# Where weight parts, x and the inner activations start within an SBUF partition: other pads in a split-fp32 transformer kernel

## The chip, the cores and the metric

The kernel runs on one core of one Trainium2 chip, in one launch. The metric is the device time of that launch in microseconds (us).

## What is computed

Two blocks follow each other on 256 tokens of width 1024. The first has two layers of feed-forward, mixer, feed-forward; the second has a two-directional recurrent mixer and a layer of retrieved experts. Cut to what matters:

```
x = x + 0.5 * swiglu(rmsnorm(x, g1), w_gate, w_up, w_down)      # D_FF = 2816, twice a layer, 2 layers
x = x + concat(attn_a, attn_b, attn_c)(rmsnorm(x, g) @ w_in) @ w_out
x = x + 0.5 * swiglu(rmsnorm(x, g2), ...)
...
x = x + g1 * token_mixer(norm(x), norm(ctx))                    # second block, one layer
x = x + g2 * peer_ffn(norm(x))     # 8 heads choose 16 of 128 x 128 experts each:
                                   # sum of g * gelu(u_tab[idx] . x) * v_tab[idx]
return rms_norm(x, norm_f_g)
```

The result is compared in fp32, and the kernel computes the experts densely: all 16,384 rows of `u_tab` and `v_tab` are multiplied, and a matrix of gates picks what counts.

## The kernel before

**One product, three matmuls.** fp32 weights come from DRAM in pieces of 128 x 1024 (`raw`, five buffers, class `W`). ScalarE rounds a piece to fp32r (`wH`, line 218), VectorE takes the rest (`wL`, line 219), three buffers each. Activations are split likewise, into `xH` and `xL` (`split_scaled`), `hH` and `hL` (`ffn`), `cH` and `cL` (the context) or the two halves of `hl` (experts). `mm3` then issues three matmuls for each product: line 256 moves the high activations against `wH`, line 257 the low ones against `wH`, line 258 the high ones against `wL`. A matmul has a weight tile of 128 x 128 as its stationary operand and moves 256 columns, the tokens. `mm3t` (lines 265 to 267) has the roles the other way round: x is stationary, and 320 to 512 columns of weights move.

**Stages.** `run` goes through feed-forward `ffn1` and mixer of layer 0, `ffn2` of layer 0, `ffn1` and mixer of layer 1, `ffn2` of layer 1 (with the context's side work between), the second block's mixer (`latents`), and `peer`. A feed-forward first makes 22 pairs of gate and up columns (moving x; 22 x 48 matmuls), which leave `hH[:, j]` and `hL[:, j]`, then 8 output tiles over 22 inner tiles (moving h; 528 matmuls). `peer` makes queries and chooses experts while 64 `u_chunk`s of 48 matmuls move x, and ends with 64 `v_chunk`s of 48 matmuls that move `hl`.

**Order.** The code order is the order on each engine; loads go out on SP's queue, whose order is that of the code too. The side work of a feed-forward (the modulation's products) is a generator that is advanced after inner tile j > 2 and after output tiles; `hold` puts a one-element POOL copy ahead of its loads, so that they start no earlier than a given tile.

**Where a tile starts.** Tiles come from stacked pools, each pool a range of bytes in every partition, and every tile starts at a multiple of 32 bytes. `pad` takes some bytes at the start of a pool, so that what follows moves up: 96 in `s` (small things; `xH` and `xL` in the pool `b` behind it move with it), 32 in `w` (weight parts; all pools behind it move too) and 32 in `po2` (the experts' `hl` and one-hot tiles). The built program has these starts:

| tile | before, modulo 128 | before, modulo 256 | after, modulo 128 | after, modulo 256 |
|---|---|---|---|---|
| `wH`, `wL`, `raw` | 96 | 224 | 0 | 0 |
| `xH`, `xL` | 32 | 160 | 0 | 128 |
| `hH`, `hL` in order of the four calls | 32, 32, 32, 32 | 32, 32, 32, 32 | 64, 96, 0, 64 | 64, 96, 128, 64 |
| `hl` | 32 | 32 | 64 | 64 |
| `oH`, `oL` (mixers' output) | 32 | 32 | 64 | 64 |
| `cH`, `cL` | 96 | 96 | 0 | 128 |

All slices of one tile that a matmul reads start a multiple of 512 bytes apart, so the table holds for every matmul of a tile.

Of the kernel before, what the change touches and what calls it, by code (L numbers as in the profile page):

```python
# [241 lines left out]
class K:  # L242
# [142 lines left out]
        self.consts.append((self.segs[i], t))  # L385


    def ffn(self, name, l, side=iter(()), every=1, down=1):

        nc, x = self.nc, self.x  # L390
        xs = self.split_scaled(x, self.c("g_" + name, KT * l, KT * l + KT), KT)
        rb, _ = self.stats(x, KT, D)
        with self.tc.tile_pool(name="ffn", bufs=1) as fp:
            self.fp = fp
            hH = fp.tile([128, FT, T], F32R, name="hH")
            hL = fp.tile([128, FT, T], F32R, name="hL")
            for j in range(FT):
                w, self.ahead = self.ahead or W(self, self.ap[name + "_gu"][l, j], 2048, 1024), None
                w.load()
                p = self.bank().rearrange("p (a t) -> p a t", a=2)  # L400
                for a in range(2):
                    for k in range(KT):
                        self.mm3(p[:, a], w, (a * KT + k) * 128, xs, k, k == 0, k == KT - 1)
                gu = fp.tile([128, 2, T], F32, name="gu", bufs=2)
                nc.vector.tensor_tensor(gu, p, rb[:, None, :].to_broadcast([128, 2, T]), op=OP.mult)
                nc.scalar.activation(gu[:, 0], gu[:, 0], AF.Silu)
                h = gu[:, 0]
                nc.vector.tensor_tensor(h, h, gu[:, 1], op=OP.mult)
                nc.scalar.activation(hH[:, j], h, AF.Copy)
                nc.vector.tensor_tensor(hL[:, j], h, hH[:, j].bitcast(F32), op=OP.subtract)  # L410
                self.mark = h
                if j % every == 0 and j > 2:
                    self.used_late()
                    next(side, None)
                self.mark = None
            for m in range(KT):
                p = self.bank()[:, :T]
                for half in range(2):
                    w = self.wchunk(self.ap[name + "_d"][l, 2 * m + half], 1408, 768)
                    for k in range(11):  # L420
                        self.mm3(p, w, k * 128, (hH, hL), 11 * half + k, half + k == 0, half * 11 + k == FT - 1)
                nc.vector.scalar_tensor_tensor(x[:, m], p, 0.5, x[:, m], op0=OP.mult, op1=OP.add)
                self.mark = x[:, m]
                self.used_late()
                if down:
                    next(side, None)
                self.mark = None
            self.used_late()
# [1082 lines left out]
    def run(self):  # L1511
        tc, nc = self.tc, self.nc
        with ExitStack() as es:
            self.sp = es.enter_context(tc.tile_pool(name="s", bufs=1))
            self.bp = es.enter_context(tc.tile_pool(name="b", bufs=1))
            self.wp = es.enter_context(tc.tile_pool(name="w", bufs=1))
            dp = es.enter_context(tc.tile_pool(name="d", bufs=1, space=bass.MemoryType.DRAM))
            self.xd = dp.tile([128, KT, T], F32, name="xd")
            self.pad(self.sp, 96)
            self.pad(self.wp, 32)  # L1520
            self.ones = self.sp.tile([128, 128], F32, name="ones")
            nc.vector.memset(self.ones, 1.0)
            with tc.tile_pool(name="x", bufs=1) as xp, tc.tile_pool(name="q", bufs=1) as self.qp:
                self.x = xp.tile([128, KT, T], F32, name="x")
                self.load_consts(self.sp, 0)
                self.ahead = W(self, self.ap["ffn1_gu"][0, 0], 2048, 512)
                for k in range(0, KT, 2):
                    if k % 4 == 0:
                        self.ahead.load(1)
                    nc.sync.dma_start(self.x[:, k:k + 2], self.ap["xT"][:, T * k:T * k + 2 * T])  # L1530
                self.ident = self.c("ident")
                self.mod = self.sp.tile([128, 48, 2], F32, name="mod")
                self.banks = {"mm": 2, "at": 2, "s": 2, "pt": 1, "o": 1}
                with tc.tile_pool(name="g", bufs=1) as gp, \
                        tc.tile_pool(name="ps", bufs=1, space=bass.MemoryType.PSUM) as self.ps:
                    steps = self.modulation(gp)
                    side = chain(islice(steps, 6), self.later(lambda: self.load_consts(gp, 1)), steps)
                    for l in range(2):
                        if l:
                            self.ffn("ffn2", 0, side, 2, 1)  # L1540
                        self.ffn("ffn1", l, side, 2 - l, l)
                        with tc.tile_pool(name="mix", bufs=1) as self.kp:
                            self.mixer(l)
                    for _ in side:
                        pass
                with tc.tile_pool(name="g2", bufs=1) as self.g2:
                    self.banks = {"mm": 3, "at": 3, "c": 2}
                    with tc.tile_pool(name="ps1", bufs=1, space=bass.MemoryType.PSUM) as self.ps:
                        self.pb = "c"
                        with tc.tile_pool(name="ctx", bufs=1) as self.kp:  # L1550
                            side = self.context()
                            self.ffn("ffn2", 1, islice(side, STEPS))
                            xs = self.first_norm()
                            for _ in side:
                                pass
                        self.pb = "mm"
                        self.latents(xs)
                self.banks = {"mm": 4, "at": 4}
            with tc.tile_pool(name="ps2", bufs=1, space=bass.MemoryType.PSUM) as self.ps:
                self.peer()  # L1560
# [33 lines left out]
```

## Time and profile before

| | us |
|---|---|
| three runs | 2116.16, 2124.03, 2128.60 |
| median | 2124.03 |
| the profiled execution | 2126.69 |
| its span, first to last instruction | 2124.8 |

The profile gives busy times by engine, groups of equal instructions, waits, and the instructions in order of time. PE is the matmuls, PEld the weight loads that run beside them. Matmuls are pipelined: one is recorded for some 280 ns while the next starts some 115 ns later, so what counts for the time is the distance from start to start, which the timeline shows directly, or a dense stretch's length divided by the matmuls in it. A window's count includes matmuls that began before it and reach into it.

### The profile page before, as it was taken

How to read it: one execution, taken by the hardware profiler on the slowest of the kernel's cores; microseconds unless marked ns; L12 is line 12 of the kernel's file. 1: busy time of each engine (PE TensorE's matmuls, PEld its weight loads, DVE VectorE, ACT ScalarE, POOL GpSimd, SP SyncE). 2: the span in 40 equal slices, each digit the busy share in tenths (PEclk: the TensorE clock that was granted, in tenths of full speed). 3: DMA queues.
4: the chain of work that ended last, by engine and by line, in shares of the span. 5: the costliest groups of instructions: out<-in, count | busy, mean ns of one | idle time of the engine just before them, and what ended most of it. 6: DMA issues, size and time to landing. Idle time of an engine off the chain costs nothing. (4 is left out here: it accounts for less than half of the span.)

```text
span 2124.8 us, 43280 instructions
## 1 busy us (share of the span) xinstructions
PE 2069.4 (97%) x17204; PEld 2011.8 (95%) x17204; DVE 1590.4 (75%) x3211; ACT 1161.3 (55%) x2011; POOL 38.9 (2%) x148
## 2 busy tenths in 40 slices
PE   8999999999999999999999998999999999999997
PEld 8999989999999998998997898999999999999997
DVE  7776977888787797777758868888888885555555
ACT  5544465444444445557446645545588874444444
POOL 0001000001000100000000000000000000000000
PEclk9999999999999999999999999999999999999998
DMA  7666535768777753555463434555545455555553
GB/s 233 224 211 189 155 101 165 227 215 256 237 261 252 246 161 95 162 182 168 154 194 119 146 113 154 187 193 181 171 160 166 163 170 188 189 186 185 186 188 120
DMA packets 115115, 385.38 MB, mean 181 GB/s; under 512 B 12768, under 2 KB 13920, under 8 KB 114784
## 3 DMA queue, kind: packets, MB, share of 16 engines
q1 hardware_dynamic: 114912, 382.61, 56.0%
q8 instruction: 135, 2.21, 0.4%
q14 instruction: 68, 0.56, 0.1%
HBM read 380.46 MB, written 2.10 MB: 180 GB/s over the span
## 5 line engine op out<-in xcount | busy, mean ns | idle before, releaser
L219 DVE TENSOR_TENSOR wL<-raw,wH 128x1024 fp32r<-128x1024 f32 (+3 forms) x716 | 812.5, 1138 | 368.5 <-ACT wH L218 366.7
L218 ACT ACTIVATE wH<-raw 128x1024 fp32r<-128x1024 f32 (+3 forms) x716 | 707.2, 990 | 679.4 <-PE mm L257 464.2
L256 PE MATMUL mm<-xH,wH 128*128 128x256 f32 x2952 | 833.3, 283 | 10.1 <-ACT xH L360 6.2
L258 PE MATMUL mm<-xH,wL 128*128 128x256 f32 x2952 | 828.7, 281 | 7.4 <-DVE wL L219 7.2
L257 PE MATMUL mm<-xL,wH 128*128 128x256 f32 x2952 | 828.3, 281 | 1.1 <-DVE xL L361 0.5
L256 PEld LDWEIGHTS mm<-xH,wH 128*128 128x128 f32 x2952 | 558.8, 189 | 13.4 <-ACT xH L360 6.7
L258 PEld LDWEIGHTS mm<-xH,wL 128*128 128x128 f32 x2952 | 561.3, 190 | 10.2 <-DVE wL L219 9.1
L257 PEld LDWEIGHTS mm<-xL,wH 128*128 128x128 f32 x2952 | 560.3, 190 | 4.2 <-DVE xL L361 1.8
L257 PE MATMUL mm<-hl,wH 128*128 128x256 f32 x1024 | 286.7, 280 | 0.0
L256 PE MATMUL mm<-hl,wH 128*128 128x256 f32 x1024 | 285.7, 279 | 0.0
L258 PE MATMUL mm<-hl,wL 128*128 128x256 f32 x1024 | 285.7, 279 | 0.0
L258 PE MATMUL mm<-hH,wL 128*128 128x256 f32 x704 | 196.8, 280 | 1.2 <-DVE wL L219 1.2
L257 PE MATMUL mm<-hL,wH 128*128 128x256 f32 x704 | 196.8, 280 | 0.0
L256 PE MATMUL mm<-hH,wH 128*128 128x256 f32 x704 | 196.6, 279 | 0.0
L256 PEld LDWEIGHTS mm<-hl,wH 128*128 128x128 f32 x1024 | 192.5, 188 | 0.0
L257 PEld LDWEIGHTS mm<-hl,wH 128*128 128x128 f32 x1024 | 192.2, 188 | 0.0
L258 PEld LDWEIGHTS mm<-hl,wL 128*128 128x128 f32 x1024 | 191.5, 187 | 0.0
L258 PEld LDWEIGHTS mm<-hH,wL 128*128 128x128 f32 x704 | 131.9, 187 | 1.6 <-DVE wL L219 1.6
L256 PEld LDWEIGHTS mm<-hH,wH 128*128 128x128 f32 x704 | 132.1, 188 | 0.0
L257 PEld LDWEIGHTS mm<-hL,wH 128*128 128x128 f32 x704 | 132.1, 188 | 0.0
L740 DVE SCALAR_TENSOR_TENSOR prod<-wm,cv 128x1024 f32<-128x1024 f32 x64 | 78.4, 1226 | 31.6 <-DMA wm<-wmod 17.4
L1339 ACT ACTIVATE o<-o,gL 128x128 f16<-128x128 f16 x256 | 85.7, 434 | 11.3 <-DVE o L1333 8.0
(466 smaller groups left out, 2507.6 us busy)
## 6 DMA issues: line engine op xcount, KB each, us to landing
raw<-ffn_gu SPq DMA_DIRECT2D x174, 512.0 KB, 4.7
raw<-ut SPq DMA_DIRECT2D x128, 512.0 KB, 4.1
raw<-vt SPq DMA_DIRECT2D x128, 512.0 KB, 4.0
raw<-win SPq DMA_DIRECT2D x58, 512.0 KB, 4.6
wm<-wmod SPq DMA_DIRECT2D x48, 512.0 KB, 5.3
raw<-ffn_d SPq DMA_DIRECT2D x64, 384.0 KB, 3.5
raw<-ffn_d SPq DMA_DIRECT2D x64, 320.0 KB, 3.3
raw<-wout SPq DMA_DIRECT2D x24, 512.0 KB, 3.7
```

The costliest lines, as they stand in the source:

```text
L218: k.nc.scalar.activation(H[:, :n], raw[:, :n], AF.Copy)
L219: k.nc.vector.tensor_tensor(L[:, :n], raw[:, :n], H[:, :n].bitcast(F32), op=OP.subtract)
L256: mm(out, H, xH[:, k], start=first, stop=False, skip_group_check=skip)
L257: mm(out, H, xL[:, k], start=False, stop=False, skip_group_check=skip)
L258: mm(out, L, xH[:, k], start=False, stop=last, skip_group_check=skip)
L740: nc.vector.scalar_tensor_tensor(out, raw, 1.0, cv[:, D * i:D * i + D], op0=OP.mult, op1=OP.mult, accum_out=self.mod[:, j, i:i + 1])
L1339: nc.scalar.activation(o[:, 3, i // 2, :, i % 2], o[:, 1, i // 2, :, i % 2], AF.Copy, scale=wL[:, 4 * u + i:4 * u + i + 1])
```

## The change

`ffn` gets an argument `pad`, and takes that many bytes at the start of its pool: none in the first and the last call, 32 in `ffn2` of layer 0, 64 in `ffn1` of layer 1. The pad of `s` goes from 96 to 64 bytes, that of `w` from 32 to 96. The table above has what that makes of the starts. Nothing else is changed; the memset that fills a pad is the only instruction that is added, two of them.

```diff
-    def ffn(self, name, l, side=iter(()), every=1, down=1):
+    def ffn(self, name, l, side=iter(()), every=1, down=1, pad=0):
...
         with self.tc.tile_pool(name="ffn", bufs=1) as fp:
             self.fp = fp
+            if pad:
+                self.pad(fp, pad)
             hH = fp.tile([128, FT, T], F32R, name="hH")
             hL = fp.tile([128, FT, T], F32R, name="hL")
...
-            self.pad(self.sp, 96)
-            self.pad(self.wp, 32)
+            self.pad(self.sp, 64)
+            self.pad(self.wp, 96)
...
                     for l in range(2):
                         if l:
-                            self.ffn("ffn2", 0, side, 2, 1)
-                        self.ffn("ffn1", l, side, 2 - l, l)
+                            self.ffn("ffn2", 0, side, 2, 1, 32)
+                        self.ffn("ffn1", l, side, 2 - l, l, 64 * l)
```

POOL's instructions where `ffn2` of layer 0 ends and `ffn1` of layer 1 begins (`wm` and `prod` are the modulation's tiles that `hold` marks, `x` and `gu` what they are held for), the program after against the one before:

```order
 L378 COPY prod<-x 128x1
 L378 COPY wm<-x 128x1
+L373 MEMSET pad_6777 128x16
 L378 COPY wm<-gu 128x1
 L378 COPY prod<-gu 128x1
```

The line with + is the pad of `ffn1` of layer 1; `ffn2` of layer 0 has its own further up in the same way, between `kc<-kr` and `wm<-gu`. On PE, VectorE, ScalarE and SP the order of instructions is the same as before.

## Rows read from the trace of the kernel before

**Rows 1.** The page: busy time of each engine; TensorE's granted clock by slice.

```profile
PE 2069.4 (97%) x17204; PEld 2011.8 (95%) x17204; DVE 1590.4 (75%) x3211; ACT 1161.3 (55%) x2011; POOL 38.9 (2%) x148
PEclk9999999999999999999999999999999999999998
```

**Rows 2.** Groups kept apart by form: count, busy us and mean ns, idle before.

```profile
L256 PE MATMUL mm<-xH,wH 128*128 128x256 f32 x2952 | 833.3, 283 | 10.1 <-ACT xH L360 6.2 <-DVE x L709 1.3 <-ACT wH L218 0.8
L256 PE MATMUL at<-xH,wH 128*128 128x256 f32 x128 | 35.8, 285 | 1.7 <-ACT xH L792 1.7
L219 DVE TENSOR_TENSOR wL<-raw,wH 128x1024 fp32r<-128x1024 f32 x546 | 665.7, 1222 | 298.6 <-ACT wH L218 297.9
L256 PE MATMUL mm<-hl,wH 128*128 128x256 f32 x1024 | 285.7, 279 | 0.0
L256 PE MATMUL mm<-hH,wH 128*128 128x256 f32 x704 | 196.6, 279 | 0.0
```

**Rows 3.** Dense stretches of x, PE alone: us, busy (matmuls), clock, DMA share, GB/s.

```profile
24.00:132.00 108.00, 108.00 (x956) 1.00 0.68 222
355.00:471.00 116.00, 116.00 (x987) 1.00 0.68 219
548.00:607.00 59.00, 59.00 (x503) 1.00 0.72 242
888.00:924.00 36.00, 36.00 (x309) 1.00 0.65 224
1344.00:1364.00 20.00, 20.00 (x179) 1.00 0.53 175
1431.00:1457.00 26.00, 26.00 (x223) 1.00 0.56 184
...
1557.00:1743.00 186.00, 128.04 (x463) 1.00 0.50 165
```

**Rows 4.** Groups in 1344 to 1364 us, then in 548 to 607 us.

```profile
L257 PE MATMUL mm<-xL,wH 128*128 128x256 f32 x59 | 16.3, 276 | 0.0
...
L257 PE MATMUL mm<-xL,wH 128*128 128x256 f32 x168 | 47.2, 281 | 0.0
```

**Rows 5.** Timeline (start, us), first and late `hl`; groups in 1749.2 to 2105 us.

```profile
1749.16 0.28 PE L256 MATMUL mm<-hl,wH 128*128 128x256 f32 x1
...
2104.62 0.28 PE L256 MATMUL mm<-hl,wH 128*128 128x256 f32 x1
...
L256 PE MATMUL mm<-hl,wH 128*128 128x256 f32 x1008 | 281.2, 279 | 0.0
```

**Rows 6.** Timeline where the first feed-forward goes from x to `hH`.

```profile
131.53 0.28 PE L258 MATMUL mm<-xH,wL 128*128 128x256 f32 x1
...
132.32 0.28 PE L256 MATMUL mm<-hH,wH 128*128 128x256 f32 x1
...
132.91 0.28 PE L258 MATMUL mm<-hH,wL 128*128 128x256 f32 x1
```

**Rows 7.** Timeline behind a stall of the router's products.

```profile
1422.28 0.39 PE L258 MATMUL at<-xH,wL 128*128 128x256 f32 x1 [0.19 <-DVE wL L219]
1422.50 0.28 PE L256 MATMUL at<-xH,wH 128*128 128x256 f32 x1
...
1423.67 0.28 PE L257 MATMUL at<-xL,wH 128*128 128x256 f32 x1
```

**Rows 8.** Timeline, c's products, then x.

```profile
1023.88 0.28 PE L256 MATMUL c<-cH,wH 128*128 128x256 f32 x1
...
1026.73 0.28 PE L256 MATMUL mm<-xH,wH 128*128 128x256 f32 x1
```

**Rows 9.** The pads' memsets on POOL.

```profile
L373 POOL MEMSET pad<- x3: 104/104/118, 0.7 to 1540.9; 128x8 f32 x2, 128x24 f32 x1
```

**Rows 10.** Stretches as in rows 3: a down-projection, the experts.

```profile
471.00:533.00 62.00, 62.00 (x529) 1.00 0.80 250
1749.00:2111.00 362.00, 362.00 (x3075) 1.00 0.56 182
```

## The prediction

> **What bounds the kernel now.** I read the page first. TensorE's matmul row is busy 97% of the span, its weight loads 95%, VectorE 75%, ScalarE 55%, and the granted clock is full in every slice [rows 1]. So the time is the number of matmuls by what one of them takes, and nothing off TensorE has to be made shorter. The second reading is the costliest groups kept apart by form [rows 2]: 3 x 2,952 and 3 x 128 matmuls move `xH` or `xL` (9,240), 3 x 1,024 move `hl` (3,072), 3 x 704 move `hH` or `hL` (2,112). All are 256 columns against a 128x128 weight tile, one instruction form, some 14,400 of the 17,204.
>
> The third reading is what this change is about: how far apart two such matmuls start. I take dense stretches, divide their length by the matmuls that began in them (a count of [rows 3] holds about two that began before the stretch), and find two levels. Moving x: 108 us hold 954, so 113.2 to 113.3 ns; 116 us hold 985, so 117.8 ns; 59 us hold 501, so 117.8 ns; the 20 us from 1344 hold 177, 113.0 ns, and the 26 us from 1431 hold 221, 117.6 ns [rows 3]. Taken the same way, 1373 to 1393 us counts as 1344 to 1364 does, and 1460 to 1486 and 1490 to 1516 us as 1431 to 1457 does, within one. The recorded duration tells the two levels apart as well: 276 ns in the first kind of stretch, 281 in the second [rows 4], with the same clock of 1.00, the same line, the same tiles. Moving `hl` there is one level: the first starts at 1749.16 us and the line 256 that starts at 2104.62 us is the last but one of 1,008 of that line, so 1,006 rounds of three later: 355.46 us for 3,018, 117.8 ns throughout [rows 5]. All 2,112 of `hH` and `hL` go the same way, 279 to 280 ns each [rows 2], and the boundary shows it without any gap: the last seven steps up to the first `hH` take 0.79 us, 113 ns each, and the five behind it 0.59 us, 118 ns [rows 6]. The step at the boundary comes with the moved tile and no wait, so something about the tiles, their place, sets the spacing. The same x tile at the same place has both levels, and changes level behind a stall: behind the 0.19 us wait at 1422.28 us ten steps take 1.17 us, 117 ns, where 1344 to 1364 us had 113 [rows 3, 7]. So place is not all; what came before counts too.
>
> A third kind, moving `cH` and `cL`, is slower still: 24 matmuls from 1023.88 to 1026.73 us, 118.75 ns [rows 8]. In the layout of before the weight parts start at 96 modulo 128, x, `hH`, `hL` and `hl` at 32, `cH` and `cL` at 96: c is the only shown tile that stands where the weights stand.
>
> **The change part by part.** *The pads themselves.* Two memsets are new, on POOL, and two have another size. One costs 104 to 118 ns [rows 9] on an engine that is busy 2% [rows 1]. Behind each stand POOL's small copies that hold back the next loads of the side work; nobody waits for the pad, and the copies of a feed-forward come only after its fourth group of columns, some 20 us later. Without that cover it would be 2 x 0.1 us. Bound: 0 to +0.2 us; I take 0. No other engine's order changes, and no transfer.
>
> *Weights from 96 to 0, x from 32 to 0.* What no row shows is any matmul of this form with both at 0 modulo 128. Nearest rows: x against the weights as now (113.2 and 117.8 ns, 52 of 100 at the lower level: in the stretches of [rows 3] 954 + 177 + 177 and, where one-hot products stand between and line 257 alone is counted, about 3 x 463, against 985 + 501 + 307 + 221 + 221 + 222) and c, which stands at the same offset as the weights and takes 118.75 ns. Bounds for x: all at the lower level, 48% of 9,240, 4,435, by the step of 117.8 - 113.3 = 4.5 ns (4.45 before rounding) = -19.7 us; all at c's, 4,805 x 5.4 + 4,435 x 1.0 ns = +30.4 us. I take the nearest by name, x as it is now on the whole: 0.
>
> *`hH`, `hL` and `hl`.* These move to 64, 96, 0, 64 and 64, and the weights move under them. They are at the upper of x's two levels in every stretch. Lower bound: the 113.3 ns that the same instruction reaches on x; 3,072 x 4.45 = 13.7 us for the experts, 2,112 x 4.45 = 9.4 us for the four down-projections. Upper bound: c's 118.75, 5,184 x 1.0 = +5.2 us. I take the lower end. The reason is asymmetry: x takes either level by what came before, so a new layout deals anew for everything, and these tiles, which now draw the worse of x's two levels in every stage, have 23.1 us to gain and 5.2 to lose. The experts decide most of it, since their stage is one run of 3,072 matmuls without a gap: whatever it enters with, it keeps (362 us, PE busy in all of it [rows 10]).
>
> *What is late next if TensorE is faster.* For 48 matmuls of a v chunk (5.44 us at 113.3) DVE splits two pieces at 1.22 us each [rows 2]; the fast x stage already runs 108 us at 113 ns with 222 GB/s and no idle PE [rows 3]. A down-projection asks most of the queues, DMA share 0.80 at 250 GB/s [rows 10]; 4% more there is 260. If that were a limit, it would take back at most 4% of two stages of 62 us, 5 us. I keep it for the range.
>
> *Sum.* Profiled execution 2126.7 us (span 2124.8, and 1.9 around it): 2126.7 - 13.7 - 9.4 + 0 = **2103.6 us**, said as 2104. That execution lies 2.7 us above the median of the three runs and inside their 2116 to 2129; I do not shift for it.
>
> **A rule against it.** First the rows: one instruction form, full clock, no recorded wait, 276 ns and 113.2 in one stretch, 281 and 117.8 in another [rows 3, 4]. The Trainium skill, page "SBUF — State Buffer", section "Who interferes with whom", gives TensorE two independent read ports, one for the moving operand and one for weight loads, and says that PE never waits on anyone; its box on cachelines puts them at 16 bytes, and every start here, before and after, is a multiple of 32. By that rule the change moves nothing and the sum is 2126.7. The trace disagrees with so plain a reading, since something does make equal matmuls unequal, but it does not show that this something is the offset modulo 128.
>
> **The rivals.**
> *All at the lower level* (x too): 2103.6 - 19.7, and the 384 of the out-projections (`oH`, `oL`; 8 x 8 tiles x 3, two layers) by 4.45 ns 1.7 more: 2082. For it: weights and x then start on the same round boundary, and 113 is a level that the chip holds for 108 us on end. Against: c, also at the weights' offset, never holds it.
> *x takes c's spacing*, on the other side: what decides would be the distance between moving tile and weights, and it becomes 0 modulo 128 for x, as it is for c. Then 2126.7 + 30.4 = 2157; less if the experts come into the lower level nevertheless (2143). It decides as soon as x's dense stretches go above 117.8. For it: c is the one row with that distance, in every stretch that I looked at. Against: c also stands at 96 and not at 0, and its row is a small sample, 24 matmuls [rows 8]. This mechanism would leave `hl` at its present distance (64) and so at its level.
> *Nothing that counts moves*: levels are dealt by stalls and by the tile's larger place. x and `hH` share 32 modulo 128 now and behave differently, which speaks for it. 2116 to 2130, as the runs of before. A mechanism beside it with the same time: the reads of the moving tile and of the weights never meet, and the levels have another origin; two levels at one and the same place (x) are for it, the step at the change of tile against. The Trainium skill's rule above ("SBUF — State Buffer", "Who interferes with whom") is that mechanism.
>
> **How the numbers follow.** h and hl at the lower level, x about as now: 0.33, 2104. All lower: 0.15, 2082. x as c: 0.32, 2143 to 2157. No net change: 0.20, 2127 (0.13 levels dealt again and as evenly, 0.07 reads that never meet). Within 0.5% (10.6 us, about what a measurement of this kernel can tell from no change) lies the last; so faster 0.48, same 0.20, slower 0.32. The likeliest case alone spans 2096 to 2110 (only the tiles at 64 profit: 13.7 + 4.7, 2108; the feed bound 5 us). The range to hold 8 in 10 reaches to both neighbours, 2083 to 2155: it leaves out the full gain and more, and the full loss.
>
> **What would show it.** In the profile after: `hl` from its first to its last start, 348 us instead of 362, with durations near 276 ns in place of 279 to 280 (the experts' 13.7 us); each down-projection 60 us in place of 62. For x, the share of stretches at 276 and 281 ns should be about even; if they read 281 and more everywhere, and the first feed-forward's 108 us become 113, the rival with c is right and the prediction wrong by up to 53 us. If the groups of `hl` stay at 280 and x keeps both, nothing moved. A new wait of PE for `wL` or raw tiles in the down-projections would be the feed.

## The result and the profile after

The changed kernel takes **2150.06 us** (median of 4 runs, 2149.31 to 2150.70) against 2124.22 us before (4 runs, 2116.16 to 2128.60): ratio 1.0124, 95% interval 1.0104 to 1.0145. It is slower by 26 us, where 2104 was forecast. Between the two profiled executions the difference is 2149.31 - 2126.69 = 22.6 us, and between their spans 2147.3 - 2124.8 = 22.5. Of the runs below, two of the ten of `e1_x_back` ran at a lower granted clock (0.56 and 0.65; 3382 and 2884 us), so its times are those of the other eight.

The page of the kernel after answers to [rows 1]: busy time of each engine, and the granted clock by slice.

```profile
PE 2099.8 (98%) x17204; PEld 2044.5 (95%) x17204; DVE 1592.4 (74%) x3211; ACT 1161.9 (54%) x2011; POOL 39.1 (2%) x150
PEclk9999999999999999999999999999999999999999
```

PE's busy time goes from 2069.4 to 2099.8 us, **+30.4**, with the same 17,204 matmuls at the same full clock, while the other engines do what they did (VectorE 1590.4 and 1592.4, ScalarE 1161.3 and 1161.9). So single matmuls became longer. The groups kept apart by form show which ones (count, busy us and mean ns of one, idle before); they answer to [rows 2].

```profile
L256 PE MATMUL mm<-xH,wH 128*128 128x256 f32 x2952 | 843.1, 286 | 10.7 <-ACT xH L360 7.1 <-DVE x L711 1.3 <-ACT wH L218 0.9
L256 PE MATMUL mm<-hl,wH 128*128 128x256 f32 x1024 | 286.0, 279 | 0.0
L256 PE MATMUL mm<-hH,wH 128*128 128x256 f32 x704 | 197.8, 281 | 0.0
```

The matmuls that move x went from 283 to 286 ns on line 256, 833.3 to 843.1 us, and lines 257 and 258 likewise (828.3 to 839.0 and 828.7 to 838.8). `hl` is where it was, 285.7 and 286.0 us; `hH` is up by 1.2 us. The distance from start to start is read as before, from dense stretches (us, busy us and matmuls in them, clock, DMA share, GB/s; two of each count began earlier). In order: x in the first feed-forward, the down-projection of `ffn2` of layer 0, x and then the down-projection in `ffn1` of layer 1, x in `ffn2` of layer 1, x in the experts, `hl`.

```profile
24.00:132.00 108.00, 108.00 (x913) 1.00 0.65 212
477.00:540.00 63.00, 63.00 (x528) 1.00 0.78 245
614.00:675.00 61.00, 61.00 (x516) 1.00 0.78 266
675.00:732.00 57.00, 57.00 (x483) 1.00 0.82 262
1043.00:1063.00 20.00, 20.00 (x169) 1.00 0.54 172
1357.00:1377.00 20.00, 20.00 (x171) 1.00 0.51 170
1773.00:2130.00 357.00, 357.00 (x3034) 1.00 0.56 183
```

- x in the first feed-forward: 108 us hold 911, 118.6 ns, where [rows 3] had 954 and 113.2. The 20 us at 1357 hold 169, 118.3 ns, where the same stage had 177. In `ffn2` of layer 1 x goes slower still: the 20 us at 1043 hold 167, 119.8 ns. So this distance, too, has more than one spacing, but none near 113.
- The two down-projections that the change moved off distance 64: 526 in 63 us are 119.8 ns (moving tile 96 behind the weights), 481 in 57 us are 118.5 (128 behind). `hl`, at 64, stays where it was: 357 us hold 3,032, 117.7 ns, as [rows 5, 10].

Not all of the 30 us reach the end. In the stage of `ffn1` of layer 1 PE had waited in the kernel before; this is nearly the same piece of work there, in the trace of before:

```profile
607.00:671.00 64.00, 60.32 (x513) 1.00 0.74 249
```

64 us with 60.3 busy before, 61 us all busy after. PE's recorded waits on line 258 for `wL` show the same; first before, then after (us in total, times, longest):

```profile
PE mm L258 <- DVE wL L219: 8.5, 9, 2.3
```

```profile
PE mm L258 <- DVE wL L219: 4.4, 3, 2.3
```

Of the 8.5 us of those waits 4.1 are gone: a slower TensorE leaves VectorE's splits more time to arrive. Together the time in which PE is not busy fell by 30.4 - 22.5 = 7.9 us; where the other 3.8 come from is not shown.

### The profile page after: what moved, and what is told of

Same layout as the page of the kernel before. It is cut to its first block, busy times and chain, and to the rows that moved or that the text cites. A ratio compares the mean times of both kernels' runs of the same rounds, so it can differ in the third digit from the quotient of the medians.

```text
span 2147.3 us, 43284 instructions
## 1 busy us (share of the span) xinstructions
PE 2099.8 (98%) x17204; PEld 2044.5 (95%) x17204; DVE 1592.4 (74%) x3211; ACT 1161.9 (54%) x2011; POOL 39.1 (2%) x150
## 5 line engine op out<-in xcount | busy, mean ns | idle before, releaser
L256 PE MATMUL mm<-xH,wH 128*128 128x256 f32 x2952 | 843.1, 286 | 10.7 <-ACT xH L360 7.1
L258 PE MATMUL mm<-xH,wL 128*128 128x256 f32 x2952 | 838.8, 285 | 4.4 <-DVE wL L219 4.4
L257 PE MATMUL mm<-xL,wH 128*128 128x256 f32 x2952 | 839.0, 284 | 0.9 <-DVE xL L361 0.4
L258 PE MATMUL mm<-hl,wL 128*128 128x256 f32 x1024 | 286.0, 279 | 0.0
L256 PE MATMUL mm<-hl,wH 128*128 128x256 f32 x1024 | 286.0, 279 | 0.0
L742 DVE SCALAR_TENSOR_TENSOR prod<-wm,cv 128x1024 f32<-128x1024 f32 x64 | 78.4, 1226 | 28.3 <-DMA wm<-wmod 14.9
```

The lines of the kernel that those rows point to most:

```text
L256: mm(out, H, xH[:, k], start=first, stop=False, skip_group_check=skip)
L257: mm(out, H, xL[:, k], start=False, stop=False, skip_group_check=skip)
L258: mm(out, L, xH[:, k], start=False, stop=last, skip_group_check=skip)
L742: nc.vector.scalar_tensor_tensor(out, raw, 1.0, cv[:, D * i:D * i + D], op0=OP.mult, op1=OP.mult, accum_out=self.mod[:, j, i:i + 1])
```

## The experiments

Distances below are the start of the moving tile less that of the weight tile, modulo 256 bytes. Before: x 192, all of `hH`, `hL` and `hl` 64, c 128. After: x and c 128; the four down-projections 64, 96, 128, 64; `hl` 64. Each ratio below is to runs of the kernel before that were made beside it, in four rounds with medians of 2122.20 (`e1` to `e4`), 2126.09 (`e5` to `e7`), 2127.43 (`e8` and `e9`) and 2124.53 us (`e10` and `e11`).

### Is it the distance, or the place?

`e1_x_back` takes the kernel after and moves x (with the small tables of pool `s`) back to its old distance; the weights stay at 0.

```diff
-            self.pad(self.sp, 64)
-            self.pad(self.wp, 96)
+            self.pad(self.sp, 128)
+            self.pad(self.wp, 32)
```

> The kernel after, with the pad of s at 128 and that of w at 32: weights stay at 0 modulo 256, the inner activations where the change put them, and only what lies in the pools s and b moves, xH and xL from 128 to 192. Theory D (the distance from the weight tile to the moving tile decides; alignment by itself does nothing): x is 192 behind the weights again, as in the kernel before, so its matmuls come back to a mix of 113.3 and 117.8 ns (mean near 115.5) and the time to 2116 to 2131 us. Theory A (weights, or both, at the start of a 128-byte line are what slows x): weights still stand at 0, x stays near 118.8 ns, time 2145 to 2151 us.

`e2_x_alone` takes the kernel before and moves x alone, in the same way, to distance 128; the weights stay at 224.

```diff
-            self.pad(self.sp, 96)
-            self.pad(self.wp, 32)
+            self.pad(self.sp, 32)
+            self.pad(self.wp, 96)
```

> The kernel before, with the pad of s at 32 and that of w at 96: weights stay at 224 modulo 256, all other tiles at their places, and only x moves, from 160 to 96, to a distance of 128 from the weights. Theory D: x goes to about 118.8 ns everywhere as c does, +3.3 ns for each of some 9,000 matmuls, 2146 to 2152 us, although nothing stands at the start of a 128-byte line. Theory A: nothing is at 0, so x keeps its mix and the time is 2116 to 2131 us.

`e1_x_back`: 2127.90 us, ratio to the kernel before 1.0024 (1.0003 to 1.0044). `e2_x_alone`: 2147.77 us, 1.0123 (1.0086 to 1.0161). Dense stretches of x in the first and the second feed-forward, of `e1_x_back` (with those of its second and third down-projections behind them) and then of `e2_x_alone`:

```profile
24.00:132.00 108.00, 108.00 (x955) 1.00 0.67 223
355.00:470.00 115.00, 115.00 (x979) 1.00 0.65 218
473.00:536.00 63.00, 63.00 (x528) 1.00 0.81 256
663.00:726.00 63.00, 63.00 (x528) 1.00 0.82 263
```

```profile
24.00:132.00 108.00, 108.00 (x913) 1.00 0.64 213
360.00:470.00 110.00, 110.00 (x928) 1.00 0.65 216
```

With x back at 192 both levels are there again, 953 in 108 us (113.3 ns) and 977 in 115 us (117.7); with x at 128 there are neither, 911 in 108 us (118.6) and 926 in 110 us (118.8), although neither x nor the weights start at 0 modulo 128 in that kernel. Theory A falls, since x has its old levels with the weights at 0 and loses them with nothing at 0, and moving x by 64 bytes is almost all of the 26 us. Theory D fits both runs. What `e1_x_back` keeps of the change, the pads of the feed-forwards, puts its second and third down-projections at 526 in 63 us, 119.8 ns, and so costs 2 x 528 x (119.8 - 117.8) ns = 2.1 us; its interval of +0.6 to +9.3 us holds that. (The third, at distance 128, took 118.5 ns in the kernel after: the second spacing of this distance again.)

A rival stays beside theory D: that the start of the moving tile counts by itself, wherever the weights are. Both runs move x and hold the weights, and no run moves the weights alone. For the distance speaks that x starts at 160 and at 192 with the same two levels when both are 192 from the weights (the kernel before and `e1_x_back`), and at 128 and at 96 with the same 118.6 ns when both are 128 from them (the kernel after and `e2_x_alone`). The third down-projection starts at 128 in the kernel after and in `e5_scan` below, and takes 118.5 ns at distance 128 and 117.3 at 160. So the distance is the reading that fits all rows, and the role of the weights in it rests on comparisons between kernels.

### What other distances do

`e5_scan` puts the four down-projections of the kernel before at distances 0, 32, 160 and 224 (and `hl` at 192). The diff is against the kernel after; the pads of `s` and `w`, left out here, are 96 and 32 as in the kernel before.

```diff
-                            self.ffn("ffn2", 0, side, 2, 1, 32)
-                        self.ffn("ffn1", l, side, 2 - l, l, 64 * l)
+                            self.ffn("ffn2", 0, side, 2, 1, 224)
+                        self.ffn("ffn1", l, side, 2 - l, l, (192, 96)[l])
...
-                            self.ffn("ffn2", 1, islice(side, STEPS))
+                            self.ffn("ffn2", 1, islice(side, STEPS), pad=160)
...
-            self.pad(op2, 32)
+            self.pad(op2, 160)
```

> The kernel before, with pads of 192, 224, 96 and 160 bytes in the four feed-forwards, so that their inner activations stand at distances of 0, 32, 160 and 224 from the weights, and with hl at 192. The kernel after had 118.66 ns at a distance of 128 and 119.99 ns at 96. If the distance counts modulo 128, the first down-projection takes 118.7 to 120 ns a matmul, the last 120, and the second and third the same as each other, at a spacing that no run has shown yet. If it counts modulo 256, 0 and 128 differ, and so do 96 and 224. Time: 2116 to 2135 us.

2129.77 us, 1.0016 (1.0001 to 1.0031). Stretches within the four down-projections:

```profile
135.00:195.00 60.00, 60.00 (x502) 1.00 0.66 193
475.00:535.00 60.00, 60.00 (x517) 1.00 0.81 252
665.00:705.00 40.00, 40.00 (x343) 1.00 0.85 267
1058.00:1118.00 60.00, 60.00 (x509) 1.00 0.65 191
```

500 in 60 us are 120.0 ns at distance 0; 515 in 60, 116.5 at 32; 341 in 40, 117.3 at 160; 507 in 60, 118.3 at 224. None of the four comes near 113. Modulo 128 would make 32 and 160 the same, and 96 (119.8) and 224; they differ, by 0.8 and 1.5 ns, as modulo 256 has it. (0 and 128 can't tell, since 128 reads 118.5 or 119.8.) Yet 64 and 192 stand out as a pair.

`e6_x_32` moves x of the kernel before to distance 32.

```diff
-            self.pad(self.sp, 96)
-            self.pad(self.wp, 32)
+            self.pad(self.sp, 192)
+            self.pad(self.wp, 192)
```

> The kernel before, with 192 bytes of pad in s and in w: only x moves, to 0 modulo 256, 32 from the weights. A moving tile 32 or 160 behind the weights has been in no run. If 64 is the only distance modulo 128 that has the lower level, x takes 118 to 120 ns and the time is 2140 to 2160 us; if 32 has it without the second level, x takes 113.3 ns everywhere and the time is 2098 to 2106 us.

2134.13 us, 1.0040 (1.0024 to 1.0055), between the two times expected: x runs at 116.6 in most of its stretches. The rows are x and the down-projection of the first feed-forward, then of the next:

```profile
24.00:134.00 110.00, 110.00 (x945) 1.00 0.65 214
136.00:194.00 58.00, 58.00 (x514) 1.00 0.69 202
360.00:470.00 110.00, 110.00 (x945) 1.00 0.69 222
472.00:530.00 58.00, 58.00 (x495) 1.00 0.81 247
```

943 in 110 us twice is 116.6 ns for x. The second row was the surprise: `hH` and `hL`, at their old distance 64, run 512 in 58 us, **113.3 ns**, and in the next feed-forward 493 in 58, 117.6. So distance 64 can hold the lower level. How the first got into it from an x at 116.6 is not known.

### What decides between the two levels

`e3_x_64` puts x of the kernel before at 64, where `hH`, `hL` and `hl` are.

```diff
-            self.pad(self.sp, 96)
-            self.pad(self.wp, 32)
+            self.pad(self.sp, 224)
+            self.pad(self.wp, 160)
```

> The kernel before, with the pad of s at 224 and that of w at 160: only x moves, by 128 bytes, from 160 to 32 modulo 256, so that it stands at the same distance from the weights (64) as hH, hL and hl do, which run at 117.8 ns everywhere. If the distance counts modulo 128 (D128), x keeps both levels, mean near 115.5 ns, 2116 to 2131 us. If it counts modulo 256 and 64 is a slow distance while 192 has both levels (D256), x runs at 117.8 ns everywhere: about 2.3 ns more for 9,000, 2140 to 2148 us.

2137.96 us, 1.0070 (1.0037 to 1.0102), between the two times expected. x in the second and in the third feed-forward:

```profile
360.00:470.00 110.00, 110.00 (x936) 1.00 0.66 218
554.00:615.00 61.00, 61.00 (x541) 1.00 0.72 250
```

934 in 110 us, 117.8; 539 in 61, 113.2. Both levels exist at 64. At 64 the profiled execution has more of the upper one than at 192 in the kernel before, and all five runs are slower than the slowest of the 20 runs of it (2135.04 to 2141.29 us against 2131.69).

`e4_h_192` moves `hH`, `hL` and `hl` (with the one-hot tiles in the same buffers) to 192, x's own distance; `e7_hl_192` moves `hl` and the one-hot tiles alone, and has only the last of these edits. The diff is again against the kernel after, with the pads of `s` and `w` back at 96 and 32.

```diff
-                            self.ffn("ffn2", 0, side, 2, 1, 32)
-                        self.ffn("ffn1", l, side, 2 - l, l, 64 * l)
+                            self.ffn("ffn2", 0, side, 2, 1, 128)
+                        self.ffn("ffn1", l, side, 2 - l, l, 128)
...
-                            self.ffn("ffn2", 1, islice(side, STEPS))
+                            self.ffn("ffn2", 1, islice(side, STEPS), pad=128)
...
-            self.pad(op2, 32)
+            self.pad(op2, 160)
```

> The kernel before, with 128 bytes of pad in each feed-forward's pool and 160 in place of 32 in that of the experts: hH, hL and hl move from 32 to 160 modulo 256, the place and the distance (192) that x has. D256 (192 can have the lower level, 64 can't): the down-projections and the experts go at either level, each keeping the one that x before it ended at; the first down-projection, behind a fast x, at 113.3; time 2101 to 2126 us. D128: no difference from the kernel before in place, they stay at 117.8 ns, 2116 to 2131 us. If the level is handed on from x and the jump by 128 bytes at the boundary is what lost it, the first down-projection and any behind a fast x is fast, and those behind a slow x stay slow.

> The kernel before, with 160 bytes of pad for the experts' tiles in place of 32: hl moves from 32 to 160 modulo 256, to the distance (192) that x has. Handing on (a tile at the same distance modulo 256 keeps the level that the last one ended at; a jump by 128 bytes loses the lower one): in executions whose last u chunk is fast, the 3,072 matmuls of hl go at 113.3 ns and the time is 13.7 us less, so the runs spread down to 2102 us; in the profiled one, hl has the level of the last u chunk. If the down side of the experts is slow by its own nature, hl stays at 117.8 ns behind a fast u chunk too, and the runs spread as the kernel's before do, 2116 to 2132 us.

2124.53 us, 1.0001 (0.9976 to 1.0027), and 2127.51 us, 1.0009 (0.9992 to 1.0027): no difference, and in the profiled executions the case that would have told, a fast x ahead of a moved tile, did not occur. In `e4_h_192` x was at the upper level at the end of x's part in all four feed-forwards, and its down-projections stayed there. In `e7_hl_192` the last u chunk was slow, and `hl` behind it too. The timeline of that boundary (start, us, engine, line):

```profile
1752.56 0.28 PE L256 MATMUL mm<-xH,wH 128*128 128x256 f32 x1
...
1753.62 0.28 PE L256 MATMUL mm<-hl,wH 128*128 128x256 f32 x1
...
1754.56 0.28 PE L258 MATMUL mm<-hl,wL 128*128 128x256 f32 x1
```

Nine steps to the first `hl` in 1.06 us, eight behind it in 0.94: 118 on both sides. Moving the one-hot tiles with `hl` had changed the u chunks before it: they went fast and slow in turn, the last one slow, where the kernel before has them all fast. The last two of them, 46 matmuls in 5.2 us and then 44:

```profile
1741.60:1746.80 5.20, 5.20 (x48) 1.00 0.42 150
1748.10:1753.30 5.20, 5.20 (x46) 1.00 0.76 243
```

This is more than a chance draw, as the traces of all these kernels show. With x at distance 192 and the one-hot tiles at 64, each of the last 31 u chunks is fast in all five kernels (the one before, `e1_x_back`, and `e8` to `e10` below). With the one-hot tiles at 192 they go in turn in all three (`e4_h_192`, `e5_scan`, `e7_hl_192`). With x and the one-hot tiles at 64, in `e3_x_64`, all 31 are slow; with x at 64 and the one-hot tiles at 192, in `e11_all_64` below, the last 32 are five slow ones and then go in turn, the last one fast. So what the one-hot products between two chunks read has a part in the level of the next; by what mechanism is open. The next kernels keep the one-hot tiles at 32 and move `hl` alone. `e8_hl_split`:

```diff
-                o = op2.tile([128, 4, 2, 128, 2], F16, name="o", tag="tmp", bufs=2)
+                o = op2.tile([128, 2176], F16, name="o", tag="tmp", bufs=2)[:, :2048].rearrange("p (n b i t) -> p n b i t", n=4, b=2, t=2)
...
-                hl = op2.tile([128, 4, T], F32R, name="hl", tag="tmp", bufs=2)
+                hl = op2.tile([128, 4 * T + 64], F32R, name="hl", tag="tmp", bufs=2)[:, 32:32 + 4 * T].rearrange("p (k t) -> p k t", t=T)
```

> The kernel before, with the experts' hl alone moved from 32 to 160 modulo 256 and the one-hot tiles, which share its buffers, left at 32. In the kernel before, whose one-hot tiles stand there, all u chunks of the last stretch ran at 113.3 ns; with the one-hot tiles at 160 (the run with hl at 192 and its tiles all moved) they went 113.3 and 117.8 in turn, and the last was slow. Handing on: the last u chunk is fast, hl enters at the lower level at its own distance 192 and keeps it, 13.7 us less than the kernel before, 2103 to 2118 us. Own nature (the experts' down side is slow for another reason, its order of weights or sums): hl 117.8 ns behind a fast u chunk, 2116 to 2132 us.

`e10_wide_64` has the same wide buffers, and `hl` at their start, at its old distance 64. Against `e8_hl_split`:

```diff
-... name="hl", tag="tmp", bufs=2)[:, 32:32 + 4 * T].rearrange(...
+... name="hl", tag="tmp", bufs=2)[:, :4 * T].rearrange(...
```

> The kernel before with the experts' two shared buffers widened by 256 bytes as in the run that moved hl alone, but with hl left at 32 modulo 256, 64 from the weights. Handing on: the u chunks end fast at distance 192, hl enters at 64 and falls to 117.8 ns, 2116 to 2132 us as the kernel before. If the wider buffers, and not the distance, made hl fast, it is fast here too, 2105 to 2118 us.

`e11_all_64` turns it round: x moved to 64 (the pads of `e3_x_64`), `hl` left at 64, and the one-hot tiles moved by the 128 bytes that x moved. Against `e8_hl_split`, whose `hl` starts 128 bytes into its buffer:

```diff
-            self.pad(op2, 32)
+            self.pad(op2, 160)
...
-            self.pad(self.sp, 96)
-            self.pad(self.wp, 32)
+            self.pad(self.sp, 224)
+            self.pad(self.wp, 160)
```

> x moved to 64 from the weights as in the run with x at 64, hl left at 64, the one-hot tiles moved by the same 128 bytes as x. Handing on (the same distance for x and hl is what counts, not 192): if the u chunks of the last stretch are fast, hl is fast at its old place 32, 348 us for its 3,072, and the time is 2100 to 2125 us; the share of fast stretches of x is dealt by the stalls. If only 192 can hold the lower level from x to hl, hl stays at 117.8 ns behind a fast last u chunk, 2116 to 2141 us. If the last u chunk is slow the run does not tell.

`e8_hl_split`: **2112.52 us, 0.9936 (0.9917 to 0.9955)**. `e10_wide_64`: 2124.90 us, 1.0003 (0.9987 to 1.0018). `e11_all_64`: 2124.76 us, 1.0007 (0.9987 to 1.0027). Timeline at the boundary from the last u chunk to `hl`, and a stretch of `hl` behind it, for `e8_hl_split`:

```profile
1747.42 0.28 PE L256 MATMUL mm<-xH,wH 128*128 128x256 f32 x1
...
1748.44 0.28 PE L256 MATMUL mm<-hl,wH 128*128 128x256 f32 x1
...
1749.35 0.28 PE L258 MATMUL mm<-hl,wL 128*128 128x256 f32 x1
```

```profile
1751.00:2091.00 340.00, 340.00 (x3002) 1.00 0.59 191
```

for `e10_wide_64`:

```profile
1754.63 0.28 PE L256 MATMUL mm<-xH,wH 128*128 128x256 f32 x1
...
1755.65 0.28 PE L256 MATMUL mm<-hl,wH 128*128 128x256 f32 x1
...
1756.59 0.28 PE L258 MATMUL mm<-hl,wL 128*128 128x256 f32 x1
```

```profile
1757.00:2107.00 350.00, 350.00 (x2974) 1.00 0.57 187
```

and for `e11_all_64`:

```profile
1758.99 0.28 PE L256 MATMUL mm<-xH,wH 128*128 128x256 f32 x1
...
1760.01 0.28 PE L256 MATMUL mm<-hl,wH 128*128 128x256 f32 x1
...
1760.91 0.28 PE L258 MATMUL mm<-hl,wL 128*128 128x256 f32 x1
```

```profile
1761.00:2101.00 340.00, 340.00 (x3002) 1.00 0.60 192
```

In all three the last nine x matmuls take 1.02 us, 113 ns each. Behind them `hl` keeps that where it stands at x's distance, 0.91 and 0.90 us for eight, and 340 us hold 3,000 (113.3) in `e8_hl_split` (both 192) and in `e11_all_64` (both 64, `hl` at its old place). In `e10_wide_64` (192, then 64) it falls to 0.94 us for eight and 2,972 in 350 us (117.8). So neither 192 nor the wide buffers make `hl` fast: **a level is handed on where the distance stays the same, and the lower one is lost at a jump of 128 bytes**. The traces of all kernels have 23 boundaries from x to a down-projection or `hl` at the same distance, 5 at the lower level and 18 at the upper, and all keep their level; the lower level met a jump of 128 bytes at 10, and was lost at each. The weights stand at 224 in all 23, so the same distance is also the same start there. `e11_all_64` gives its 13.7 us back in x, which had the upper level in the first three feed-forwards of that execution (934 in 110 us in the first and the second, 722 in 85 in the third). The times agree: `e3_x_64`, with x at the same place and a slow `hl`, is 16 us above the kernel before, `e11_all_64` 0.2.

`e9_hl_h_192` adds the pads of `e4_h_192` in the feed-forwards to `e8_hl_split`.

> The same, and 128 bytes of pad in each feed-forward, so that hH and hL too stand at 192 as x does. Handing on: each down-projection behind an x that ends fast goes at 113.3 ns, 2.35 us less for each, those behind a slow x stay at 117.8; 2096 to 2116 us in all, below the run with hl alone by 2 to 5 us in the median. Own nature: as the kernel before.

**2109.24 us, 0.9917 (0.9892 to 0.9943)**, the best of all; its 3.3 us below `e8_hl_split` are as expected, though the intervals overlap, so that the times alone do not show them. The first two feed-forwards, x and then the down-projection, and a stretch of the third down-projection:

```profile
24.00:132.00 108.00, 108.00 (x955) 1.00 0.68 222
133.00:192.00 59.00, 59.00 (x523) 1.00 0.68 202
355.00:468.00 113.00, 113.00 (x962) 1.00 0.68 219
469.00:530.00 61.00, 61.00 (x520) 1.00 0.81 251
669.00:720.00 51.00, 51.00 (x452) 1.00 0.85 269
```

x at 113.3 (953 in 108 us) hands 113.2 to the down-projection (521 in 59); x at 117.7 (960 in 113) hands it 117.8 (518 in 61). These two pairs are the rule in four rows: it hands on the upper level as well as the lower.

## Why the prediction was wrong

**What bounds the kernel** was read rightly: the time is the number of matmuls by their spacing. PE's busy time carries the whole change, and both levels of x were there again wherever it stood at 192 or 64. The result lies within the stated range of 2083 to 2155, but on the other side of no change than the likeliest case; it falls to the rival with c, 0.32 and 2143 to 2157, whose sign came as told: the first feed-forward's 954 matmuls of x, 108 us before, take 113 at 118.6 ns.

**x, taken at 0, was some +27.** This is the step that failed. The bounds were -19.7 and +30.4 us, and the upper one came from c, the only row at the distance that x would have. I took "the nearest by name", x as it was; the nearest by what the change alters was c. With x moved alone, the page of `e2_x_alone` has PE busy for 2096.6 us, +27.2; with the whole change it is +30.4. The rival with c took 30.4 for x and said 2157 as its full price; what it lacked is the waits: 7.9 us came back because a slower PE waited less, over half of it for `wL`. 2157 - 7.9 = 2149, where the profiled execution is. That it meets it so closely is luck in part: the rival's 30.4 is for x alone, which cost 27.2, and the measured 30.4 has the down-projections and other tiles in it. The forecast priced what is late next if TensorE gets faster, but not what is early if it gets slower.

**`hH`, `hL` and `hl`, taken at -23.1, were +1.4.** The reason given was that a new layout deals anew for everything. But the text itself said, under the rival with c, that `hl` keeps its present distance of 64, and so do two of the four down-projections; x ahead of them stands at another distance, before (192) as after (128), so it hands them nothing. They had 117.8 ns before and after. The lower end itself, 113.3 ns, is real: `e8_hl_split` has it for all 3,072, and the time fell by 14.9 us (2127.43 to 2112.52) against a forecast term of 13.7; some of the down-projections get it in `e6_x_32` and `e9_hl_h_192`. The size was right and the cause wrong: what brings it is not new starts, but the distance of an x that ends at the lower level. The two down-projections that did move, to 96 and 128, went above 117.8, to 119.8 and 118.5.

**The pads** cost little by what the page shows (POOL busy 38.9 us before, 39.1 after; no run has them alone), and **the feed** never became the limit: at 269 GB/s and a DMA share of 0.85 the third down-projection of `e9_hl_h_192` holds 450 in 51 us, 113.3 ns.

**Reads that never meet.** Equal matmuls at the same clock take 113.3 to 120.0 ns with the place of the moving tile against the weights: `e2_x_alone` moves x and the small tables of `s`, and x's 113.3 and 117.8 ns become 118.6 to 118.8. The Trainium skill, "SBUF — State Buffer", "Who interferes with whom", has the two reads of PE on independent ports and PE waiting for no one; these runs speak against the second half in this form. Whether it is the ports, the memory behind them or the array that waits, no run here shows.

**The spread.** The four runs after lie within 1.4 us, those of the kernel before within 12, and the profiles give a possible reason: at 128 x has no level near 113, at 192 a pause can change its level, as at 1422 us in the kernel before [rows 7]. It is not shown: the four runs of `e2_x_alone`, with x at 128 too, are 6.3 us apart.

**Open:** what at a pause chooses the level, beyond the part of the one-hot tiles, and why x at 64 has the upper one more often; whether the weights' own start counts other than through the distance, which a run that moves the weights alone would tell. No kernel here forces x to the lower level; in `e9_hl_h_192` too, the whole second feed-forward ran at 117.7.

## What to carry over

- Before moving a tile, compare the start of the moving tile with that of the stationary one, not each with a round number: here 64 and 192 modulo 256 were the only distances that reached 113.3 ns, and distances of 0 modulo 128 took 118.3 to 120.
- Where a spacing has two levels, look at what a stage inherits: give tiles that follow each other without a gap the same distance, and the lower level is kept where it is there. That took 18 us off here (2127.43 to 2109.24), by moving `hH`, `hL` and `hl` alone.
- A bound from the row with the same changed quantity outranks one from the row with the same name.

## What was not expected of the hardware

- Spacing of one matmul form (256 columns, full clock) by distance modulo 256: 0: 120.0; 32: 116.6; 64: 113.3 or 117.8; 96: 119.8; 128: 118.3 to 118.8 in most stretches, and 119.8 for x in `ffn2` of layer 1 of the kernel after and in the third down-projection of `e1_x_back`; 160: 117.3; 192: 113.3 or 117.8; 224: 118.3 ns.
- The two levels at 64 and 192 last for whole stages, 3,072 matmuls on end, and are changed by pauses and by jumps of the distance.
- Tiles that other matmuls read in between matter too: with one-hot tiles moved by 128 bytes, the u chunks behind them went fast and slow in turn, in all three kernels that did this with x at 192.
